# Conformer block on one core: the mixer's order of chunks, its split low parts and the first weight chunk are changed

## The chip, the cores and the metric

The kernel runs as one program on one core of a Trainium2 chip. The metric is the device time of one execution, in microseconds (us). Before the change it is 655.03 us, the median of 3 runs (653.3 to 655.46).

## The reference, cut to what matters

One layer of a hybrid block on `x` of 256 rows by 1024, fp32. There are three stages: a gated feed-forward (2816 wide), a mixer of convolution and attention, and a second feed-forward.

```python
def hybrid_layer(x, ...):
    x = x + 0.5 * swiglu(rms_norm(x, ffn1_norm), ffn1_w_gate, ffn1_w_up, ffn1_w_down)
    h = rms_norm(x, mix_norm)
    proj = h @ w_in                                  # 7 sections of 1024 columns
    conv_a, conv_b, q, k, v, gate_a, gate_b = jnp.split(proj, SPLITS, axis=-1)
    u = conv_a * jax.nn.sigmoid(conv_b)
    u = causal_depthwise_conv(u, conv_dw, conv_dw_bias)   # 31 taps
    u = jax.nn.silu(layer_norm(u, conv_ln_gain, conv_ln_bias))
    y_a = u @ w_conv_proj
    q = rms_norm(q.reshape(b, s, 16, 64), q_norm)    # per head
    k = rms_norm(k.reshape(b, s, 16, 64), k_norm)
    y_b = moba_attention(q, k, v) @ w_attn_proj
    mixed = jax.nn.sigmoid(gate_a) * y_a + jax.nn.sigmoid(gate_b) * y_b
    x = x + mixed @ w_out
    x = x + 0.5 * swiglu(rms_norm(x, ffn2_norm), ffn2_w_gate, ffn2_w_up, ffn2_w_down)
    return x
```

With 256 rows and blocks of 256, `moba_attention` is causal softmax attention within the one block: scores times 64 ** -0.5, a causal mask, softmax, times v.

## The kernel before, in words

Every large product is one `gemm` (L97): 256 rows as two halves `t`, a chunk of 512 weight columns, and k-tiles of 128. Weights come in pieces of two k-tiles (512 KB) through SyncE's queue (SP) into one of five `raw` buffers. `split` (L89) then makes two fp32r parts: ScalarE casts `raw` to `hi` (L91), and VectorE, or GpSimd where `pool_lo` is set, subtracts to get `lo` (L93). TensorE runs three matmuls for each k-tile and half: high by `hi` (L133), high by `lo` (L134), low by `hi` (L135). So a piece is 12 matmuls and a chunk of eight k-tiles is 48. A `raw` buffer is free for the next load when its low part is made. The two sums of a chunk lie in `acc`, of which there are three.

FFN 1 has 11 chunks of gate and up columns (`hTh`, `hTl` on the left) and two chunks of the down product with 22 k-tiles (`aTh`, `aTl`); FFN 2 is the same on `h2h`, `h2l`. Rows are normalised late: the product is taken on x times the gain, and the row factor `rstd` enters as the scale of the Silu (L237) and in the gated product (L260).

At the start, `start` (L533) loads x transposed, in four transfers between the first weight pieces. For each k-tile GpSimd squares it and adds it up (`sq`, L549, L551), ScalarE makes `hTh` (L552) and VectorE `hTl` (L553). The row sums are two small matmuls (`rstd_x`, L570). The natural x (1 MB, for the residual) and the constants are loaded after the second chunk (`load_rest`, L580).

The mixer has 14 chunks of `w_in`: b, a, b, a for the convolution (each 512 columns), then k, q, v, k, q, v, and four gate chunks. Each sum is turned to natural tiles and transposed on TensorE by functions kept in `later`, which run after the second piece of the next chunk. `conv` (L299) is 31 taps for each of eight tiles of 128 channels on VectorE (L313, L317), with its sum in PSUM. `pump` (L67) issues so many of its steps for each piece, behind the `anchor`, the last low part or score on VectorE. `attention` (L408) has 24 steps (score, flip and value for each of eight pairs of heads), which `side` issues at one step for each piece from the second k chunk on. A head's norm (`head_norm`, L369) is a copy and a square on ScalarE, a sum on VectorE (L380), `ms` on VectorE (L153), a power on GpSimd (L155) and a product on VectorE (L385). In the mixer's first 56 pieces 0.75 of the low parts go to GpSimd.

After the attention, ScalarE takes all eight sigmoids of both gates (L686), the chunks of `w_attn` run on `oh`, `ol`, and between the second of them and `w_conv` stands `conv_act` (L345): transposes of the normalised convolution, Silu (L359), and the parts `u2h`, `u2l`.

The tile framework orders the instructions of each engine by a simulated timeline; each engine then takes them in that order.

Of the kernel before, what the change touches and what calls it, by code (L numbers as in the profile page):

```python
# [17 lines left out]
P = 128  # L18
S = 256
# [18 lines left out]
B8_BUFS = 13  # L38
SIDE = 1.0, 1.0
PUMP = 3, 3.5, 3, 8  # L40
# [4 lines left out]
class Build:  # L45
# [16 lines left out]

    def tr(self):
# [33 lines left out]
    def gemm(self, w, c, n, kt, ah, al, pump=0, pool=0.0, first=False, split_k=None,  # L97
             side=None, before=None):
# [9 lines left out]
        for kp in sizes:  # L108
            ahead = before(k0) if before is not None else None
# [7 lines left out]
            step = 1 if first else 2
            for s in range(0, kp, step):
                e = min(s + step, kp)
                self.share += pool  # L120
                pool_lo = self.share >= 1.0
                if pool_lo:
                    self.share -= 1.0
                self.split(
                    raw[:, s * n : e * n], hi[:, s * n : e * n], lo[:, s * n : e * n], pool_lo
                )
# [22 lines left out]
    def rsqrt_mean(self, ss, n, width):  # L149
# [3 lines left out]
        nc.vector.tensor_scalar(ms, ss, 1.0 / n, EPS, ALU.mult, ALU.add)  # L153
# [17 lines left out]
    def to_T(self, src, hi, lo, k0, gain=None):  # L171
# [3 lines left out]
        ps = self.tr()
        for j in range(2):
            for t in range(2):
                nc.tensor.transpose(  # L178
                    ps[:, j * S + t * P : j * S + (t + 1) * P], src(t, j), self.ident
                )  # L180
        return self.split_T(ps, hi, lo, k0, 2, gain)
# [30 lines left out]
    def ffn(self, wgu, wd, hT, rstd_of, x, emit, tail=None, before=None, after=None):  # L212
# [9 lines left out]
        for i, n in enumerate(widths):  # L222
            last = i == len(widths) - 1
            if not last:
                if before is not None and i == 0:
                    g = self.gemm(
                        wgu, c, n, KD, ah, al, first=True, split_k=(1, 1), before=before
                    )
# [36 lines left out]
            def transp(av=av, off=off, n=n):  # L265
                for j in range(0, n // P, 2):
                    k = off // P + j
                    self.to_T(
                        lambda t, q: av[t][:, (j + q) * P : (j + q + 1) * P],
                        aTh[k // 8], aTl[k // 8], k % 8,  # L270
                    )
# [11 lines left out]
    def residual_T(self, x_new, ss, hi, lo, gain):  # L283

        def transp(c):
            for j in (0, 2):
                self.to_T(
                    lambda t, q: x_new[:, t * D + c * CH + (j + q) * P : t * D + c * CH + (j + q + 1) * P],
                    hi, lo, c * 4 + j, gain,
                )  # L290
# [8 lines left out]
    def conv(self, uT, tiles):  # L299
# [3 lines left out]
        for c0 in tiles:  # L303
# [510 lines left out]
```

## Time and profile before

| | |
|---|---|
| time, median of 3 runs | 655.03 us (653.3 to 655.46) |
| the profiled execution | 653.98 us, of which 652.2 us are the span |
| mean granted TensorE clock | 0.996 |
| TensorE busy | 640.5 us (98%), 2956 matmuls and transposes |
| VectorE busy | 413.1 us (63%) |
| ScalarE busy | 342.6 us (53%) |
| GpSimd busy | 132.5 us (20%) |
| DMA | 114.98 MB, mean 176 GB/s |

The span runs from the first to the last instruction of the profiled execution. Busy time is the union of an engine's instructions; a matmul counts as busy to its modelled end, which lies after the start of the next one, so a short wait between matmuls does not show as idle time. In lists of groups the columns are line, engine, operation, names (out, then in), shapes and count, then busy us and the mean ns of one, then the idle time of the engine just before them with what ended it. Where a stretch is tabled by windows, each engine has its busy us and, in brackets, its instructions.

### The profile page before, as it was taken

What the parts mean: (1) busy time and instruction counts of PE and PEld (TensorE: products, weight loads), DVE (VectorE), ACT (ScalarE), POOL (GpSimd) and SP (SyncE); (2) the same over time, 40 slices, a digit from 0 to 9 for tenths busy, and PEclk for the clock granted to TensorE, in tenths of its full rate; (3) what the DMA queues carried; (4) which work ended last, traced back from release to release, by engine and by line L of the source; (5) the groups of instructions that cost most, each with busy time, mean ns of one, the idle gap of its engine ahead of it and who ended that gap; (6) DMA issues with size and microseconds to landing.
All of it is one profiled execution on the core that took longest, in us unless ns stands there. A gap on an engine that the chain in (4) does not pass through costs nothing.

```text
span 652.2 us, 8131 instructions
## 1 busy us (share of the span) xinstructions
PE 640.5 (98%) x2956; PEld 519.8 (80%) x2956; DVE 413.1 (63%) x664; ACT 342.6 (53%) x512; POOL 132.5 (20%) x80
## 2 busy tenths in 40 slices
PE   7999999999999999999999999999999999999997
PEld 5788888888888888877777777788888888888886
DVE  5764636455532399999989874775754546455541
ACT  5543545354534645668665685943654535454330
POOL 6300000000025667847744400000000000000000
PEclk8999999999999999999999999999999999999999
DMA  8865655647565556444454433365655666656740
GB/s 275 315 224 164 193 193 173 216 132 233 163 213 163 183 175 219 144 153 134 156 162 130 162 124 102 130 207 179 197 171 182 193 194 182 189 162 204 206 124 32
DMA packets 33000, 114.98 MB, mean 176 GB/s; under 512 B 3648, under 2 KB 5056, under 8 KB 32960
## 3 DMA queue, kind: packets, MB, share of 16 engines
q1 hardware_dynamic: 32960, 114.46, 54.8%
q8 instruction: 23, 0.38, 0.3%
q14 instruction: 17, 0.14, 0.1%
HBM read 113.40 MB, written 1.05 MB: 175 GB/s over the span
## 4 chain that ended last, share of the span: by engine, by line
PE 90%; DVE 3%; ACT 3%; DMA 1%; issue 1%; SPq 0%; DVEq 0%; ACTq 0%
PE acc L134 28%; PE acc L133 28%; PE acc L135 28%; PE tr L178 2%; PE tr L423 1%; DMA raw<-w1gu 1%; PE tr L481 1%; DVE cv L317 1%; DVE lo L93 1%; ACT hi L91 1%; PE tr L466 1%; ACT gate L686 1%; ACT pr L445 0%; DVE hxn L385 0%; PE tr L397 0%
## 5 line engine op out<-in xcount | busy, mean ns | idle before, releaser
L91 ACT CAST hi<-raw 128x1024 fp32r<-128x1024 f32 (+1 forms) x216 | 222.9, 1037 | 242.1 <-PE acc L135 217.3
L93 DVE TENSOR_TENSOR lo<-raw,hi 128x1024 fp32r<-128x1024 f32 (+1 forms) x174 | 217.2, 1253 | 182.1 <-ACT hi L91 177.2
L93 POOL TENSOR_TENSOR lo<-raw,hi 128x1024 fp32r<-128x1024 f32 x42 | 100.9, 2421 | 219.4 <-ACT hi L91 219.2
L317 DVE SCALAR_TENSOR_TENSOR cv<-uT,cst,cv 128x255 f32<-128x255 f32 (+26 forms) x240 | 94.4, 463 | 0.1
L134 PE MATMUL acc<-lo,h1h 128*128 128x512 f32 x224 | 88.3, 394 | 0.0
L135 PE MATMUL acc<-hi,h1l 128*128 128x512 f32 x224 | 87.5, 394 | 0.0
L133 PE MATMUL acc<-hi,h1h 128*128 128x512 f32 x224 | 87.2, 394 | 0.0
L133 PE MATMUL acc<-hi,hTh 128*128 128x512 f32 x176 | 68.8, 397 | 2.9 <-ACT hi L91 2.9
L134 PE MATMUL acc<-lo,hTh 128*128 128x512 f32 x176 | 69.9, 397 | 0.7 <-DVE lo L93 0.7
L133 PE MATMUL acc<-hi,h2h 128*128 128x512 f32 x176 | 69.2, 393 | 0.0
L135 PE MATMUL acc<-hi,hTl 128*128 128x512 f32 x176 | 69.0, 393 | 0.0
L133 PE MATMUL acc<-hi,aTh 128*128 128x512 f32 x176 | 68.7, 391 | 0.0
L135 PE MATMUL acc<-hi,aTl 128*128 128x512 f32 x176 | 68.5, 389 | 0.0
L134 PE MATMUL acc<-lo,aTh 128*128 128x512 f32 x176 | 68.5, 389 | 0.0
L134 PE MATMUL acc<-lo,h2h 128*128 128x512 f32 x176 | 68.5, 390 | 0.0
L135 PE MATMUL acc<-hi,h2l 128*128 128x512 f32 x176 | 67.2, 390 | 0.0
L133 PEld LDWEIGHTS acc<-hi,h1h 128*128 128x128 f32 x224 | 42.1, 188 | 10.4 <-issue 1.3
L134 PEld LDWEIGHTS acc<-lo,h1h 128*128 128x128 f32 x224 | 42.1, 188 | 9.6 <-issue 0.7
L135 PEld LDWEIGHTS acc<-hi,h1l 128*128 128x128 f32 x224 | 42.1, 188 | 8.5 <-issue 0.3
L133 PEld LDWEIGHTS acc<-hi,hTh 128*128 128x128 f32 x176 | 33.4, 191 | 10.3 <-ACT hi L91 3.6
L134 PEld LDWEIGHTS acc<-lo,hTh 128*128 128x128 f32 x176 | 33.5, 190 | 8.9 <-DVE lo L93 2.2
L155 POOL TENSOR_TENSOR rs<-ms,neghalf 128x8 f32<-128x8 f32 (+2 forms) x13 | 17.2, 1324 | 109.7 <-DVE ms L153 109.4
(131 smaller groups left out, 783.8 us busy)
## 6 DMA issues: line engine op xcount, KB each, us to landing
raw<-w_in SPq DMA_DIRECT2D x56, 512.0 KB, 3.5
raw<-w2gu SPq DMA_DIRECT2D x44, 512.0 KB, 4.4
raw<-w1gu SPq DMA_DIRECT2D x43, 512.0 KB, 5.0
raw<-w1d SPq DMA_DIRECT2D x22, 512.0 KB, 4.2
raw<-w2d SPq DMA_DIRECT2D x22, 512.0 KB, 4.3
raw<-w_attn SPq DMA_DIRECT2D x8, 512.0 KB, 4.0
raw<-w_conv SPq DMA_DIRECT2D x8, 512.0 KB, 3.5
raw<-w_out SPq DMA_DIRECT2D x8, 512.0 KB, 4.5
```

The lines of the kernel that those rows point to most:

```text
L91: nc.scalar.copy(hi, raw)
L93: ins = eng.tensor_tensor(lo, raw, hi.bitcast(F32), ALU.subtract)
L133: nc.tensor.matmul(o, ah(k, t), wh, start=st, stop=False)
L134: nc.tensor.matmul(o, ah(k, t), wl, start=False, stop=False)
L135: nc.tensor.matmul(o, al(k, t), wh, start=False, stop=sp)
L155: nc.gpsimd.tensor_tensor(r, ms, self.neghalf[:, :width], ALU.pow)
L178: nc.tensor.transpose(ps[:, j * S + t * P : j * S + (t + 1) * P], src(t, j), self.ident)
L317: nc.vector.scalar_tensor_tensor(o, i, w, o, ALU.mult, ALU.add)
L423: nc.tensor.matmul(ps[q][:, t * P : t * P + (t + 1) * P], qT[r, b * S + t * P : b * S + (t + 1) * P], kT[r, b * S : b * S + (t + 1) * P], ...
L466: nc.tensor.transpose(ps[:, i * P : (i + 1) * P], pr[:, o : o + P], self.ident)
L481: nc.tensor.matmul(ps[q * HD : (q + 1) * HD, kt * P : S], v[:, kt * D + h * HD : kt * D + (h + 1) * HD], pT[:, o : o + n], start=kt == 0, ...
L686: last = nc.scalar.activation(g[:, sl], g[:, sl], AF.Sigmoid)
```

## The change

- **Start.** `gemm_first` replaces the first chunk: one transfer brings a k-tile's 512 weight columns and the 256 columns of x transposed that belong to it (3 KB per partition), and the sums lie in the two `cv` tiles. GpSimd's squares and the four sum matmuls go. `rstd_x` now runs after the second chunk: it loads the natural x, squares it on ScalarE (four `sum_squares`) and takes the power as elsewhere. The `ms` step of every norm goes from VectorE to ScalarE.
- **Order.** The convolution's chunks hold 256 b and 256 a columns each, so one chunk gives two tiles. They stand at places 0, 1, 5 and 9 of the 14, with k, q, v of the first heads at 2 to 4 and of the others at 6 to 8, and the gates last. The attention is issued at 0.75 steps for each piece from place 5 and 0.95 from place 9.
- **Low parts.** From the second chunk on, and in `w_attn`, every low part is GpSimd's: 60 instead of 42.
- **Head norms.** q is not normalised; its factor, with 64 ** -0.5 in it, enters as the scale of the exponential and in its bias `nb`. The row maxima lie in PSUM.
- **Convolution.** The first tap of each tile goes to ScalarE; its steps are no longer tied behind the anchor.
- **Tail.** The sigmoids of the second gate come after the Silu of `conv_act`, and `conv_act` comes ahead of the second `w_attn` chunk.

```diff
-B8_BUFS = 13
-SIDE = 1.0, 1.0
-PUMP = 3, 3.5, 3, 8
+B8_BUFS = 12
+W_IN = [
+    ("u", 0), ("u", 1), ("k", 0), ("q", 0), ("v", 0), ("u", 2), ("k", 1), ("q", 1), ("v", 1),
+    ("u", 3), ("b", 0), ("b", 1), ("a", 0), ("a", 1),
+]
+SIDE = [0] * 5 + [0.75] * 4 + [0.95] * 5
+NORM_AT = "a", 0
+PUMP = 3.5, 4
+POOL_LO = 1.0
...
-        with self.tc.issue_after(self.anchor.ins) if self.anchor else nullcontext():
+        with nullcontext():
             while self.credit >= 1 and self.bg:
...
+    def gemm_first(self, x0, w0, rest, hT):
...
+        acc = [self.cv(), self.cv()]
...
+        for k in range(KD):
+            raw = self.wp.tile([P, KP * CH], F32, tag="raw", name="raw", bufs=RAW_BUFS)
+            hi = self.wp.tile([P, KP * CH], F32R, tag="hi", name="hi", bufs=HI_BUFS)
+            lo = self.wp.tile([P, KP * CH], F32R, tag="lo", name="lo", bufs=LO_BUFS)
+            if k == 0:
+                nc.sync.dma_start(x0, self.io["x0"])
+                nc.sync.dma_start(raw[:, :CH], w0)
+                xk = x0[:, KD:]
+            else:
+                self.last_dma = nc.sync.dma_start(raw[:, : CH + S], rest[:, k - 1, :])
+                xk = raw[:, CH : CH + S]
+            g = x0[:, k : k + 1]
+            sl = slice(k * S, (k + 1) * S)
+            nc.scalar.activation(hTh[:, sl], xk, AF.Copy, scale=g)
+            nc.vector.scalar_tensor_tensor(
+                hTl[:, sl], xk, g, hTh[:, sl].bitcast(F32), ALU.mult, ALU.subtract
+            )
+            self.split(raw[:, :CH], hi[:, :CH], lo[:, :CH], False)
+            for t in range(2):
+                o, st, sp = acc[t], k == 0, k == KD - 1
+                nc.tensor.matmul(o, ah(k, t), hi[:, :CH], start=st, stop=False)
+                nc.tensor.matmul(o, ah(k, t), lo[:, :CH], start=False, stop=False)
+                nc.tensor.matmul(o, al(k, t), hi[:, :CH], start=False, stop=sp)
+        return acc
...
-        nc.vector.tensor_scalar(ms, ss, 1.0 / n, EPS, ALU.mult, ALU.add)
+        nc.scalar.activation(ms, ss, AF.Copy, bias=EPS, scale=1.0 / n)
...
-                        nc.vector.tensor_scalar(
-                            o, i, w, cst[:, C_CB + c : C_CB + c + 1], ALU.mult, ALU.add
-                        )
-                    else:
-                        nc.vector.scalar_tensor_tensor(o, i, w, o, ALU.mult, ALU.add)
...
+                    nc.scalar.activation(
+                        o, u, AF.Identity, bias=cst[:, C_CB + c : C_CB + c + 1], scale=w
+                    )
+                else:
+                    nc.vector.scalar_tensor_tensor(o, u, w, o, ALU.mult, ALU.add)
...
+            if rq is not None:
+                ms = self.tmp.tile([P, 8], F32, tag="ms8", name="ms", bufs=2)
+                nc.scalar.activation(ms, ss, AF.Copy, bias=HD * EPS)
+                nc.gpsimd.tensor_tensor(rq[:, :, t], ms, self.neghalf, ALU.pow)
+                xs.append(x)
+                continue
...
-            mx = self.tmp.tile([P, 4], F32, tag="mx", name="mx", bufs=2)
+            mx = ps[0][:, 3 * P : 3 * P + 4]
...
-            self.anchor = nc.vector.tensor_scalar(nb, mx, -scale, None, ALU.mult)
+            f = rq[b // 4].rearrange("p h t -> p (h t)")[:, (b % 4) * 4 : (b % 4) * 4 + 4]
+            self.anchor = nc.vector.scalar_tensor_tensor(
+                nb, mx, -1.0, f, ALU.mult, ALU.mult
+            )
...
-                        scale=scale, accum_out=sums[:, i : i + 1],
+                        scale=f[:, i : i + 1], accum_out=sums[:, i : i + 1],
...
+        def first():
+            return self.gemm_first(
+                x0, io["w1f"][: P * CH].rearrange("(p n) -> p n", n=CH),
+                io["w1f"][P * CH :].rearrange("(p k n) -> p k n", p=P, n=CH + S), (hTh, hTl),
+            )
...
         def rstd_x():
...
-            sums = self.tr()
-            for t in range(2):
-                nc.tensor.matmul(
-                    sums[:, t : t + 1], sq[:, t * P : (t + 1) * P], self.ones[:, :1],
-                    start=True, stop=True,
-                )
...
-                nc.sync.dma_start(cst, io["cst"])
                 nc.sync.dma_start(
                     x.rearrange("p (t d) -> p t d", t=2),
                     io["x"].rearrange("(t p) d -> p t d", p=P),
                 )
+                nc.sync.dma_start(cst, io["cst"])
+            for t in range(2):
+                for c in range(2):
+                    self.sum_squares(x, ss0, t, c)
+            return self.rms(ss0)
...
+        def conv_in(i, ba):
+            un = []
+            for t in range(2):
+                s = self.tmp.tile([P, CH], F32, tag="sg", name="sb", bufs=3)
+                nc.scalar.activation(
+                    s[:, :S], ba[t][:, :S], AF.Sigmoid, scale=rstd[:, t : t + 1]
+                )
+                u = self.tmp.tile([P, CH], F32, tag="av", name="un", bufs=3)
+                nc.vector.scalar_tensor_tensor(
+                    u[:, :S], ba[t][:, S:], rstd[:, t : t + 1], s[:, :S], ALU.mult, ALU.mult
+                )
+                un.append(u)
...
+        for cn, (what, c) in enumerate(W_IN):
+            if (what, c) == NORM_AT:
+                self.bg.append(self.conv_norm(uT, ynat))
+            acc = self.gemm(
+                w_in, cn, CH, KD, mh, ml, pump=PUMP[0], pool=POOL_LO if cn else 0,
+                side=(att, SIDE[cn]),
+            )
             if rstd is None:
                 rstd = self.rms(ss1)
...
+            if what == "u":
+                conv_in(c, acc)
+            elif what == "k":
+                self.head_norm(acc, rstd, c, kT, C_KN)
+            elif what == "q":
+                self.head_norm(acc, rstd, c, qT, C_QN, rq[c])
+            elif what == "v":
+                scaled(v, c, acc)
+            else:
+                if c == 0:
+                    gates.append(self.big(f"gate_{what}"))
+                scaled(gates[-1], c, acc)
...
-        with tc.issue_after(self.last_att.ins):
-            for g in (gb, ga):
+        def sigmoid(g, after):
+            with tc.issue_after(after.ins):
                 for i in range(4):
                     sl = slice(i * CH, (i + 1) * CH)
                     last = nc.scalar.activation(g[:, sl], g[:, sl], AF.Sigmoid)
+            return last
+        last = sigmoid(gb, self.last_att)
         for c in range(2):
-            acc = self.gemm(wb, c, CH, KD, ph, pl, pump=PUMP[3])
             if c:
                 self.drain()
-                self.conv_act(ynat, u2h, u2l, last)
+                sigmoid(ga, self.conv_act(ynat, u2h, u2l, last))
+            acc = self.gemm(wb, c, CH, KD, ph, pl, pump=PUMP[1], pool=POOL_LO)
```

## Rows read from the trace of the kernel before

**Rows 1.** The waits of TensorE by releaser, whole span: us in total, times, longest

```profile
PE acc L133 <- ACT hi L91: 2.9, 1, 2.9
PE acc L133 <- ACT u2h L365: 1.3, 1, 1.3
PE tr L466 <- DVE ms L153: 1.2, 1, 1.2
```

**Rows 2.** Line 133, first of three matmuls per k-tile: durations, first and last start

```profile
L133 PE MATMUL acc<-hi,h1h x224: 387/389/500, 197.5 to 383.3; 128*128 128x512 f32 x112
...
L133 PE MATMUL acc<-hi,hTh x176: 387/389/773, 4.8 to 135.6; 128*128 128x512 f32 x176
...
L133 PE MATMUL acc<-hi,aTh x176: 389/389/481, 136.3 to 647.4; 128*128 128x512 f32 x176
...
L133 PE MATMUL acc<-hi,h2h x176: 389/389/481, 462.6 to 587.1; 128*128 128x512 f32 x176
```

**Rows 3.** Windows: length, busy PE, PEld, DVE, ACT, POOL (counts), clock, DMA share, GB/s

```profile
0.00:10.00 10.00, 7.30 (x28) 5.71 (x28) 3.12 (x8) 4.22 (x8) 4.25 (x14) 1.00 0.71 209
10.00:20.00 10.00, 8.02 (x27) 5.86 (x27) 9.90 (x12) 8.49 (x14) 9.76 (x12) 0.83 0.84 306
20.00:30.00 10.00, 10.00 (x46) 8.28 (x47) 7.02 (x8) 4.31 (x5) 2.13 (x2) 1.00 1.00 369
```

**Rows 4.** The timeline, 3 to 12 us: start, us, instruction, idle before it

```profile
3.45 0.48 DVE L553 SCALAR_TENSOR_TENSOR hTl<-x,hTh 128x256 fp32r<-128x256 f32 x1 [2.41 <-ACT hTh L552]
...
6.46 0.68 DVE L93 TENSOR_TENSOR lo<-raw,hi 128x512 fp32r<-128x512 f32 x1
...
11.32 0.73 PE L133 MATMUL acc<-hi,hTh 128*128 128x512 f32 x2 [2.94 <-ACT hi L91]
```

**Rows 5.** Groups by shape on VectorE, 0 to 23 us: busy, mean ns, idle before

```profile
L93 DVE TENSOR_TENSOR lo<-raw,hi 128x512 fp32r<-128x512 f32 x8 | 8.3, 1072 | 0.9 <-ACT hi L91 0.8
L553 DVE SCALAR_TENSOR_TENSOR hTl<-xT,x,hTh 128x256 fp32r<-128x256 f32 x7 | 5.5, 817 | 2.8 <-ACT hTh L552 2.8
```

**Rows 6.** Groups by shape, whole span: what row norms and gating take

```profile
L260 DVE SCALAR_TENSOR_TENSOR av<-acc,rs,sg 128x512 f32<-128x512 f32 x20 | 14.2, 744 | 1.6 <-PE acc L135 1.6
...
L237 ACT ACTIVATE sg<-acc,rs 128x512 f32<-128x512 f32 x20 | 13.5, 687 | 8.7 <-PE acc L135 6.3 <-POOL rs L155 2.3
...
L161 ACT ACTIVATE junk<-x 128x512 f32<-128x512 f32 x8 | 5.0, 629 | 3.7 <-DVE x L723 2.7 <-DVE x L596 1.0
...
L155 POOL TENSOR_TENSOR rs<-ms,neghalf 128x2 f32<-128x2 f32 x3 | 3.0, 1008 | 76.2 <-DVE ms L153 76.2
```

**Rows 7.** Windows in the mixer, columns as in rows 3

```profile
240.00:285.00 45.00, 45.00 (x215) 36.91 (x214) 44.68 (x96) 24.70 (x34) 34.12 (x16) 1.00 0.56 182
285.00:330.00 45.00, 43.75 (x206) 32.80 (x205) 44.14 (x112) 33.10 (x70) 29.86 (x14) 1.00 0.42 139
330.00:385.50 55.50, 55.26 (x276) 41.44 (x276) 48.99 (x136) 38.44 (x90) 19.91 (x9) 1.00 0.41 131
```

**Rows 8.** Groups by shape, whole span: low parts, head norms, one table load

```profile
L93 DVE TENSOR_TENSOR lo<-raw,hi 128x1024 fp32r<-128x1024 f32 x166 | 208.9, 1262 | 181.1 <-ACT hi L91 176.3
L93 POOL TENSOR_TENSOR lo<-raw,hi 128x1024 fp32r<-128x1024 f32 x42 | 100.9, 2421 | 219.4 <-ACT hi L91 219.2
...
L155 POOL TENSOR_TENSOR rs<-ms,neghalf 128x8 f32<-128x8 f32 x8 | 13.1, 1636 | 7.9 <-DVE ms L153 7.5
...
L385 DVE TENSOR_TENSOR hxn<-hx,rs 128x512 f32<-128x512 f32 x8 | 10.2, 1280 | 0.0
...
L153 DVE TENSOR_SCALAR ms<-hss 128x8 f32<-128x8 f32 x8 | 5.1, 631 | 0.0
...
L445 ACT ACT_TABLE_LOAD x1 | 1.3, 1283 | 0.0
```

**Rows 9.** Line 93 on GpSimd: durations min/median/max, first and last start

```profile
L93 POOL TENSOR_TENSOR lo<-raw,hi x42: 2374/2402/2853, 190.6 to 366.7; 128x1024 fp32r<-128x1024 f32 x42
```

**Rows 10.** The waits of GpSimd, 200 to 280 us

```profile
POOL rs L155 <- DVE ms L153: 4.7, 4, 2.2
```

More of the change, by code (lines that the diff above doesn't have):

```diff
@@ L95, in split, with gemm @@
             self.anchor = ins
-    def gemm(self, w, c, n, kt, ah, al, pump=0, pool=0.0, first=False, split_k=None,
-             side=None, before=None):
+    def gemm_first(self, x0, w0, rest, hT):
+        nc = self.nc
+        acc = [self.cv(), self.cv()]
+        hTh, hTl = hT
+        ah, al = self.parts(*hT)
+        for k in range(KD):
[22 more added lines that the diff above has]
+        return acc
+    def gemm(self, w, c, n, kt, ah, al, pump=0, pool=0.0, split_k=None, side=None):
         nc = self.nc
@@ L112, in gemm @@
             lo = self.wp.tile([P, KP * CH], F32R, tag="lo", name="lo", bufs=LO_BUFS)
-            with self.tc.issue_after(ahead.ins) if ahead else nullcontext():
-                self.last_dma = nc.sync.dma_start(
-                    raw[:, : kp * n].rearrange("p (k n) -> p k n", n=n), w(c, k0, kp)
-                )
[L117 to L125, printed above, removed]
-                )
+            self.last_dma = nc.sync.dma_start(
+                raw[:, : kp * n].rearrange("p (k n) -> p k n", n=n), w(c, k0, kp)
+            )
+            self.share += pool
+            pool_lo = self.share >= 1.0
+            if pool_lo:
+                self.share -= 1.0
+            self.split(raw[:, : kp * n], hi[:, : kp * n], lo[:, : kp * n], pool_lo)
             for t in range(2):
@@ L169, in rms, with to_T @@
         return self.rsqrt_mean(s2, D, 2)
[L171 removed]
+    def to_T(self, src, hi, lo, k0, n, gain=None):
         nc = self.nc
[L175 to L181 removed]
+        for j in range(0, n, 2):
+            ps = self.tr()
+            for q in range(2):
+                for t in range(2):
+                    nc.tensor.transpose(
+                        ps[:, q * S + t * P : q * S + (t + 1) * P], src(t, j + q), self.ident
+                    )
+            self.split_T(ps, hi, lo, k0 + j, 2, gain)
     def split_T(self, ps, hi, lo, k0, nk, gain):
@@ L209, in parts, with ffn @@
         return ap(hi), ap(lo)
-    def ffn(self, wgu, wd, hT, rstd_of, x, emit, tail=None, before=None, after=None):
+    def ffn(self, wgu, wd, hT, rstd_of, x, emit, tail=None, first=None):
         nc = self.nc
@@ L224, in ffn @@
             if not last:
[L225 to L228, printed above, removed]
+                if first is not None and i == 0:
+                    g = first()
                 else:
@@ L265, in transp @@
             def transp(av=av, off=off, n=n):
[L266 to L271, printed above, removed]
+                k = off // P
+                self.to_T(
+                    lambda t, q: av[t][:, q * P : (q + 1) * P],
+                    aTh[k // 8], aTl[k // 8], k % 8, n // P,
+                )
             self.later.append(transp)
@@ L285, in transp @@
         def transp(c):
[L286 to L290, printed above, removed]
+            self.to_T(
+                lambda t, q: x_new[:, t * D + c * CH + q * P : t * D + c * CH + (q + 1) * P],
+                hi, lo, c * 4, 4, gain,
+            )
             for t in range(2):
@@ L392, in transp @@
         def transp():
-            for j in (0, 2):
+            for j in range(0, 4, 2):
                 ps = self.tr()
@@ L601, in run @@
         self.ffn(
-            w_of("w1gu", KD), w_of("w1d", KF), (hTh, hTl), rstd_x, x, emit_into(x1, x),
-            self.residual_T(x1, ss1, h1h, h1l, C_GM), before=start, after=load_rest,
+            w_of("w1gu", KD, first=1), w_of("w1d", KF), (hTh, hTl), rstd_x, x, emit_into(x1, x),
+            self.residual_T(x1, ss1, h1h, h1l, C_GM), first=first,
         )
@@ new lines, in scaled @@
+        def scaled(dst, c, acc):
+            for t in range(2):
+                nc.scalar.activation(
+                    dst[:, t * D + c * CH : t * D + (c + 1) * CH], acc[t], AF.Copy,
+                    scale=rstd[:, t : t + 1],
+                )
+        for cn, (what, c) in enumerate(W_IN):
[4 more added lines that the diff above has]
+                side=(att, SIDE[cn]),
+            )
```

205 lines of the change are left out of this document (72 added, 133 removed).

## The prediction

> **What bounds the kernel now.** I read the busy times first: TensorE is busy 98% of the span, the others far less, so the question is where the last 2% go. The list of TensorE's waits [rows 1] names few: 2.9 us on one cast of a weight piece, 1.3 us on the high part of the convolution's output, 1.2 us ahead of a transpose of the attention's probabilities. A wait is counted only past a matmul's modelled end, some 0.39 us after its start, though the next could start after 0.23 us, so each hides some 0.16 us more.
>
> The two feed-forwards check this. They hold the same products: from the first `hTh` matmul to the first `h1h` one is 197.5 - 4.8 = 192.7 us; from the first `h2h` to the last `aTh` with the three matmuls left there is 647.4 + 0.7 - 462.6 = 185.5 us [rows 2]. So FFN 1 loses 7.2 us. With 792 matmuls in 185.5 us the pace is 0.23 us each, transposes included, and a chunk of 48 takes 11.0 us. The 7.2 us lie in the start: between 0 and 20 us TensorE is busy 7.3 and 8.0 of 10 us, and its clock, at 2.4 GHz otherwise, is granted at 0.83 on average in the second stretch (part of it at 1.2 GHz), after the 2.94 us of idle time that end at 11.32 [rows 3, 4]. In that stretch VectorE is busy 9.90 of 10 us and GpSimd 9.76 [rows 3]. VectorE's two operations for a k-tile take 0.48 and 0.68 us at their shortest [rows 4], but 0.82 and 1.07 us on average beside GpSimd's squares [rows 5]. So the first chunk is held by late pieces first, then by VectorE.
>
> In the mixer the waits of [rows 1] are 2.5 us; with the hidden parts and smaller ones I put what can be won at 3 to 4 us. VectorE is busy 44.68 + 44.14 + 48.99 = 137.8 of 145.5 us between 240 and 385.5 [rows 7], 95%, ScalarE 96.2, GpSimd 83.9. The scores and `lo` parts queue behind convolution taps there.
>
> So nearly all of a gain must come out of 7.2 + 4 = 11 us, and the rest is 2.4 GHz matmul work that the change keeps.
>
> **Start.** Removed: 15 GpSimd operations and four sum matmuls. The bytes stay: 0.13 MB of x0, eight k-tiles of weights (2.10 MB) and the rest of x transposed (0.92 MB) are 3.15 MB. At the rates of [rows 3], 209 and then 306 GB/s, 2.09 MB are in by 10 us and the last k-tile by 10 + 1.06/0.306 = 13.5 us. A cast (taken like the low part), a low part of 0.68 us [rows 4] and six matmuls (1.4 us) put the end of the chunk at 16.2 us, against 4.8 + 11.0 = 15.8 without any wait. VectorE needs 0.48 + 0.68 = 1.16 us for a k-tile, less than TensorE's 1.4, so it no longer sets the pace. The least left over is 0.4 us. The most is 4.5 us: one idle stretch as in [rows 4] with a clock of 1.2 GHz behind it (17% of 10 us is 1.7 us). I take 1.7, since smaller pieces arrive more evenly than x and two k-tiles of weights by turns: a gain of 5.5 us, bounds 2.7 and 6.8.
>
> The row factor is late next. The natural x is issued on SP behind the second chunk's last piece; with five `raw` buffers and k-tiles that take one each, that piece waits for the seventh k-tile's low part, and FFN 1's third chunk is queued behind x on SP. x is complete after 3.15 + 2.10 + 1.05 = 6.30 MB: 5.15 MB by 20 us, the rest at 369 GB/s [rows 3], so at 23.1 us. Four squares (0.63 us), a power (1.01), the Silu (0.69) and the gated product (0.74) [rows 6] free a sum at 23.1 + 2.5 + 1.0 + 0.7 + 0.7 = 28.0, with handovers 28.5 to 29.5. TensorE asks for it when the second chunk and six matmuls of the third are done, 16.2 + 11.0 + 1.4 = 28.6 us, because the second chunk holds two of the three `acc` tiles. A wait of 0 to 1 us; it is in the 1.7.
>
> **Mixer, VectorE.** Low parts on GpSimd go from 42 to 52 + 8 = 60, so VectorE loses 18 of 1.26 us, 22.7 us [rows 8]; four `hxn` of 1.28, 5.1 us; eight `ms` of 0.63, 5.0 us [rows 8]. That is 33 us, and eight first taps more, out of a queue 95% full. Its in-order queue then has room, and scores and transposes come earlier.
>
> **Mixer, ScalarE.** It takes the taps, `ms` and more function tables. By the order of the program the tables change between sigmoid and exponential around chunks 5 and 9, and again in the tail (sigmoid, Silu, sigmoid, Silu): 11 loads instead of 5, six more of 1.283 us [rows 8], 7.7 us. ScalarE has 145.5 - 96.2 = 49 us free in the stretch, and casts run up to five pieces (some 13 us) ahead, so I cost this at nothing; without that cover a load delays a sum's release by 1.3 us. The Trainium skill, "ScalarE: Activation LUTs", section "What ACT_TABLE_LOAD costs", puts every switch at about 2.66 us with a drain; by that the six are 16 us, still under the free time. It advises grouping by table set, which this order breaks; the trace of before shows 1.283 us a load.
>
> **Mixer, GpSimd.** In the 13 chunks that it serves, 52 x 2.42 = 125.8 us, eight head norms of 1.64 are 13.1 [rows 8], and its wait for `ms`, 4.7 us for four [rows 10], 9.6 for eight: 148.5 us. TensorE has for these 13/14 of 383.3 + 2 - 197.5 [rows 2], some 174 us. It keeps up on average. Where two head norms follow each other (q, then v) its load is 9.7 + 3.3 + 2.4 = 15.4 us a chunk against some 12, 7 us over two chunks, against a lead of up to four pieces (11 us). Hidden, but the norms' powers and `ms` now share a queue with every low part.
>
> **Tail.** `conv_act` and its Silu start four sigmoids earlier and a chunk earlier, so the 1.3 us wait should go.
>
> **Sum.** I take 2.5 us of the mixer's 3 to 4, bounds 0 and 4. Profiled execution 653.98 - 5.5 - 2.5 = 646.0 us. The median of the runs shown lies 1.05 above it: **647.0 us**. All waits gone gives 653.98 - 11 + 1.05 = 644.0.
>
> **Rivals.**
> - **GpSimd becomes the bound (slower).** All low parts stand in one in-order queue. It decides when a low part takes (174 - 22.7)/52 = 2.91 us; the longest of 42 took 2.85, the median 2.40 [rows 9]. Against it: those 2.40 were measured beside a full VectorE. For it: VectorE's own low part stretches beside GpSimd (0.68 to 1.07, [rows 4, 5]), so the two do block each other, and GpSimd's share rises. At 3.2 us it costs 52 x 3.2 + 22.7 - 174 = 15 us: 653.98 - 5.5 + 15 + 1.05 = 664.5 us. The Trainium skill, "SBUF — State Buffer", section "Who interferes with whom", says that GpSimd and a VectorE operation with two SBUF inputs lock one port pair, and that whichever starts second blocks fully; the stretched low parts agree, and the steady 2.40 us say that VectorE mostly lost. Chance 0.14.
> - **The start is bound by bytes and by x.** If the first pieces stall as now, or x comes 3 us later, 4.5 us stay: 649.8 us. Chance 0.14.
> - **The mixer's waits move.** A table load or a power that stands ahead of a cast or a low part in its queue, or a score out of time, costs each some 1 to 1.4 us as in [rows 1]; with four to six of them the mixer loses 1.5 us instead of winning 2.5: 651.0 us, up to 654. Chance 0.17.
> - **Nothing moves**, because gains and new waits cancel: 653 to 657. Chance 0.07.
> - My forecast: 0.48.
>
> About 0.3% (2.0 us) is what a measurement of this kernel can tell from no change. Faster holds the forecast, the start's rival and most of the moving waits: 0.48 + 0.14 + 0.13 = 0.75. Same: 0.07 + 0.03 = 0.10. Slower: 0.14 and a remainder of 0.01, 0.15. The range reaches from 642.8, just under all waits gone, to 655.0, and leaves out the GpSimd case and part of the last.
>
> **What would show it.** Start: first `h1h` matmul at about 192 instead of 197.5; no cast or low part in TensorE's waits before 20 us; VectorE well under 9 of 10 us between 10 and 20; the clock at 1.00 there. Row factor: a wait of the third chunk on VectorE's gated product would be the rival. Mixer: VectorE near 75% between the same places, GpSimd near 85%, low parts at 2.4 us; the time from the first `h1h` to the first `h2h` matmul falls from 265 to some 262.5 us; no wait on `u2h`. The prediction fails if GpSimd's low parts top TensorE's waits, if the granted clock drops in the mixer, or if x is late by more than 3 us.

## The result, and the profile after

The changed kernel takes 646.86 us (median of 4 runs, 646.5 to 647.54) against 654.45 us (4 runs) for the kernel before, a ratio of 0.9884 with a 95% interval of 0.9867 to 0.9902. The profiled execution is 646.76 us with a span of 644.9, against 653.98 and 652.2 before.

First the starts of the first of the three matmuls of each k-tile (now L165), which cut the span into stages: first and last start, by stage.

```profile
L165 PE MATMUL acc<-hi,h1h x224: 387/389/501, 191.9 to 377.1; 128*128 128x512 f32 x112
...
L165 PE MATMUL acc<-hi,aTh x176: 389/389/476, 130.7 to 640.1; 128*128 128x512 f32 x176
L165 PE MATMUL acc<-hi,h2h x176: 387/389/479, 455.3 to 579.8; 128*128 128x512 f32 x176
```

Against [rows 2] the first `h1h` matmul comes 197.5 - 191.9 = 5.6 us earlier: that is the start. From there to the first `h2h` matmul, the mixer, it was 265.1 us and is 455.3 - 191.9 = 263.4: 1.7 us. From there to the end of the span it is 189.6 us in both. The sum is the 7.3 us by which the span is shorter.

The three windows of the start, columns as in [rows 3]:

```profile
0.00:10.00 10.00, 8.92 (x36) 7.39 (x37) 5.17 (x12) 6.81 (x13) 1.44 (x10) 1.00 0.82 272
10.00:20.00 10.00, 9.53 (x42) 7.54 (x41) 6.98 (x10) 6.04 (x10) 0.00 (x0) 1.00 0.94 318
20.00:30.00 10.00, 10.00 (x46) 8.29 (x45) 5.81 (x8) 7.85 (x16) 1.64 (x1) 1.00 0.98 369
```

TensorE is busy 8.92 and 9.53 us where it was 7.30 and 8.02, its granted clock stays at 1.00 (2.4 GHz), VectorE falls from 9.90 to 6.98 us and GpSimd from 9.76 to nothing. The groups of VectorE between 0 and 23 us show why it has room:

```profile
L102 DVE TENSOR_TENSOR lo<-raw,hi 128x512 fp32r<-128x512 f32 x8 | 5.5, 692 | 0.6 <-ACT hi L100 0.5
...
L126 DVE SCALAR_TENSOR_TENSOR hTl<-raw,x,hTh 128x256 fp32r<-128x256 f32 x7 | 3.4, 485 | 1.9 <-ACT hTh L125 1.8
```

The low part of a k-tile takes 692 ns on average, not 1072, and that of x 485, not 817 [rows 5]: the shortest times of before [rows 4] are now the mean. What follows in the timeline is the row factor:

```profile
22.19 0.63 ACT L193 ACTIVATE junk<-x 128x512 f32<-128x512 f32 x1 [1.33 <-DMA x<-x]
...
27.56 1.27 ACT L271 ACTIVATE sg<-cv,rs 128x512 f32<-128x512 f32 x2 [0.81 <-POOL rs L187]
```
```profile
25.89 1.64 POOL L187 TENSOR_TENSOR rs<-ms,neghalf 128x2 f32<-128x2 f32 x1 [23.81 <-ACT ms L185]
```

The natural x has landed by 22.19 us, and TensorE shows no wait on the Silu or the gated product behind it. The power took 1.64 us because a low part on VectorE had begun just before it (the last section has the rows).

The mixer's windows, as in [rows 7], with their sum:

```profile
240.00:285.00 45.00, 45.00 (x212) 34.38 (x211) 38.69 (x118) 35.33 (x68) 37.48 (x18) 1.00 0.52 168
285.00:330.00 45.00, 45.00 (x228) 34.72 (x227) 27.84 (x81) 38.72 (x77) 34.71 (x17) 1.00 0.44 141
330.00:385.50 55.50, 55.50 (x264) 41.57 (x264) 28.96 (x92) 39.10 (x78) 37.52 (x17) 1.00 0.50 161
sum 145.50, PE 145.50 PEld 110.66 DVE 95.49 ACT 113.16 POOL 109.71; mean PE 48.50 PEld 36.89 DVE 31.83 ACT 37.72 POOL 36.57
```

VectorE is busy 95.5 of 145.5 us (66%), before 137.8; GpSimd 109.7 (75%); TensorE shows no idle time there at all. The waits of TensorE over the whole span, and GpSimd's low parts:

```profile
PE tr L568 <- DVE idle L565: 1.1, 1, 1.1
PE acc L165 <- ACT u2h L398: 0.8, 1, 0.8
PE acc L166 <- DVE lo L102: 0.5, 1, 0.5
```
```profile
L102 POOL TENSOR_TENSOR lo<-raw,hi x60: 2355/2400/2846, 193.2 to 394.9; 128x1024 fp32r<-128x1024 f32 x60
```

Of the mixer's two waits in [rows 1], 1.2 us ahead of a transpose is gone and 1.3 us on `u2h` is 0.8: together 1.7 us, as much as the mixer gained, so what else moved there cancels out. (The 1.1 us lies ahead of the warm-up matmuls. The 0.5 us on a low part ends at 17.69 us, at the second chunk's first piece; the prediction had expected no such wait before 20 us.) Where the 0.8 us come from is in ScalarE's timeline of the tail:

```profile
389.05 0.37 ACT L220 CAST oh<-tr 128x256 fp32r<-128x256 f32 x1 [2.09 <-PE tr L524]
389.44 1.28 ACT L697 ACT_TABLE_LOAD   x1
390.73 2.20 ACT L697 ACTIVATE gate_b<-gate_b 128x512 f32<-128x512 f32 x4
...
396.67 0.59 ACT L364 COPY ynat<-tr 128x512 f32<-128x512 f32 x1
400.74 0.21 ACT L185 ACTIVATE ms<-mv 128x1 f32<-128x1 f32 x1 [3.48 <-DVE mv L370]
...
404.42 1.28 ACT L392 ACT_TABLE_LOAD   x1
406.06 1.94 ACT L392 ACTIVATE z<-tr,cst 128x256 f32<-128x256 f32 x4 [0.35 <-PE tr L385]
407.87 0.63 ACT L398 CAST u2h<-z 128x512 fp32r<-128x512 f32 x1
```

Attention's last output (389.05), gate_b's sigmoids, the convolution's norm (copies to 396.67, statistics to 400.74), the Silu table, the Silu and the `u2h` cast follow each other on ScalarE, and the last of them ends just too late.

### The profile page after: what moved, and what is told of

Its sections match the earlier page's. It is cut to its first block, busy times and chain, and to the rows that moved or that the text cites. A ratio compares the mean times of both kernels' runs of the same rounds, so it can differ in the third digit from the quotient of the medians.

```text
span 644.9 us, 8142 instructions
## 1 busy us (share of the span) xinstructions
PE 638.5 (99%) x2952; PEld 517.1 (80%) x2952; DVE 371.6 (58%) x625; ACT 365.9 (57%) x549; POOL 163.1 (25%) x83
## 3 DMA queue, kind: packets, MB, share of 16 engines
HBM read 113.40 MB, written 1.05 MB: 177 GB/s over the span
## 4 chain that ended last, share of the span: by engine, by line
PE 67%; ACT 0%; DVE 0%; issue 0%; DVEq 0%
PE acc L165 20%; PE acc L166 20%; PE acc L167 20%; PE tr L463 2%; PE tr L524 1%; PE tr L211 1%; PE tr L509 1%; PE tr L438 1%; PE tr L359 0%; PE tr L649 0%; ACT z L392 0%; PE tr L385 0%; ACT u2h L398 0%; DVE un L640 0%; DVE ot L748 0%
## 5 line engine op out<-in xcount | busy, mean ns | idle before, releaser
L102 DVE TENSOR_TENSOR lo<-raw,hi 128x1024 fp32r<-128x1024 f32 (+1 forms) x156 | 186.6, 1199 | 169.7 <-ACT hi L100 165.3
L102 POOL TENSOR_TENSOR lo<-raw,hi 128x1024 fp32r<-128x1024 f32 x60 | 142.9, 2404 | 213.2 <-ACT hi L100 213.2
L347 DVE SCALAR_TENSOR_TENSOR cv<-uT,cst,cv 128x255 f32<-128x255 f32 (+28 forms) x240 | 95.4, 469 | 10.6 <-ACT cv L343 10.4
L165 PE MATMUL acc<-hi,h1h 128*128 128x512 f32 x224 | 88.3, 399 | 0.2 <-DVE un L640 0.2
L165 PE MATMUL acc<-hi,h2h 128*128 128x512 f32 x176 | 69.1, 393 | 0.0
L165 PE MATMUL acc<-hi,aTh 128*128 128x512 f32 x176 | 68.8, 391 | 0.0
L166 PE MATMUL acc<-lo,hTh 128*128 128x512 f32 x160 | 62.4, 390 | 0.5 <-DVE lo L102 0.5
L165 PE MATMUL acc<-hi,hTh 128*128 128x512 f32 x160 | 62.2, 392 | 0.0
L167 PE MATMUL acc<-hi,hTl 128*128 128x512 f32 x160 | 62.1, 389 | 0.0
L165 PEld LDWEIGHTS acc<-hi,h1h 128*128 128x128 f32 x224 | 42.1, 188 | 11.2 <-issue 2.0
L167 PEld LDWEIGHTS acc<-hi,aTl 128*128 128x128 f32 x176 | 33.0, 188 | 6.9
L165 PEld LDWEIGHTS acc<-hi,h2h 128*128 128x128 f32 x176 | 33.0, 188 | 6.8
L165 PEld LDWEIGHTS acc<-hi,aTh 128*128 128x128 f32 x176 | 33.0, 188 | 6.8
```

The source lines that it names most:

```text
L102: ins = eng.tensor_tensor(lo, raw, hi.bitcast(F32), ALU.subtract)
L165: nc.tensor.matmul(o, ah(k, t), wh, start=st, stop=False)
L166: nc.tensor.matmul(o, ah(k, t), wl, start=False, stop=False)
L167: nc.tensor.matmul(o, al(k, t), wh, start=False, stop=sp)
L347: nc.vector.scalar_tensor_tensor(o, u, w, o, ALU.mult, ALU.add)
```

## The experiments

Ratios are to the kernel before on the same chip. The first `h1h` start and the mixer's length (first `h1h` to first `h2h` start) are read from the profile of each, in us. Before: 197.5 and 265.1; changed: 191.9 and 263.4. Times are medians, the last two columns those of one execution: it lies 0.8 us under the median in e3, 1.7 over it in e8 and 3.5 over it in e9, elsewhere within 0.3.

| kernel | us | ratio, 95% interval | `h1h` | mixer |
|---|---|---|---|---|
| e1 new start alone | 648.83 | 0.9931 (0.9918 to 0.9944) | 192.2 | 265.2 |
| e2 new mixer alone | 651.58 | 0.9966 (0.9954 to 0.9978) | 196.9 | 263.4 |
| e3 before, no squares | 652.0 | 0.9973 (0.996 to 0.9986) | 194.6 | 265.2 |
| e4 after, squares on | 649.6 | 0.9937 (0.9925 to 0.9949) | 194.8 | 263.4 |
| e5 after, old tail | 649.71 | 0.9944 (0.9931 to 0.9957) | 191.6 | 266.6 |
| e6 after, 42 low parts | 652.04 | 0.9975 (0.9967 to 0.9984) | 192.7 | 268.0 |
| e7 GpSimd loaded, free | 648.77 | 0.9928 (0.9916 to 0.9941) | 194.2 | 263.4 |
| e8 after, old chunk order | 650.23 | 0.9958 (0.9946 to 0.9971) | 192.3 | 268.1 |
| e9 GpSimd loaded, chained | 677.22 | 1.0346 (1.03 to 1.0393) | 193.0 | 296.3 |
| e10 fewer turns | 645.63 | 0.9881 (0.9866 to 0.9896) | 192.9 | 261.3 |
| e11 norm earlier | 647.35 | 0.9909 (0.9894 to 0.9923) | 192.8 | 263.4 |
| e12 low parts alone | 654.33 | 1.0005 (0.9994 to 1.0017) | 196.7 | 265.7 |

**e1 and e2: the two halves.** e1 is the kernel before with `gemm_first`, the natural x and its row factor; e2 is the changed kernel with the old `start`, squares and sum matmuls.

> The kernel before with the new first chunk and the new row factor alone; mixer and tail as before. Theory: the start gives 5.5 us by itself, a ratio of 0.9915, with the first h1h matmul at about 192 us and the mixer's 265 us unchanged. Rival: start and mixer only pay together (the mixer's waits shift when it begins earlier), then under 4 us or the mixer's length moves by over 1 us.

> The changed kernel with the start of before (squares on GpSimd, x transposed in four transfers, two-k-tile pieces). Theory: the mixer gives 1.7 us by itself, a ratio of 0.9974, first h1h matmul at about 197.5 us and 263.4 us from there to the first h2h matmul. Rival: it gives nothing alone (within 0.5 us) or 3 us and more.

The halves add up: 0.9931 x 0.9966 = 0.9897, near 0.9884, and each half's stage is as long as in the whole change to 0.3 us. So they can be studied apart.

**e3 and e4: what in the start.** e3 takes GpSimd's squares out of the old start (the row factor then comes from the natural x as in the change); e4 puts them into the new one, where nobody reads them.

```
e3 -   nc.gpsimd.tensor_tensor(sq[:, sl], src, src, ALU.mult)
   -   if j: nc.gpsimd.tensor_tensor(sq[:, :S], sq[:, :S], sq[:, sl], ALU.add)
e4 +   nc.gpsimd.tensor_tensor(self.sq[:, sl], xk, xk, ALU.mult)
   +   if k: nc.gpsimd.tensor_tensor(self.sq[:, :S], self.sq[:, :S], self.sq[:, sl], ALU.add)
```

> The kernel before without GpSimd's squares and the four sum matmuls; the row factor from the natural x after the second chunk, first sums in the two cv tiles; weight pieces and transfers of x transposed as before. Theory A (VectorE, slowed by GpSimd, holds the first chunk): 3 to 5 us faster. Theory B (the uneven arrival of pieces holds it, with the 2.9 us idle and the low clock behind it): under 1.5 us faster, the idle stretch and a granted clock under 0.9 between 10 and 20 us stay.

> The changed kernel with the 15 squares and sums on GpSimd put back beside the first chunk (their result is not used). Theory A: VectorE's 1.16 us for a k-tile become 1.9 us, over TensorE's 1.4, so the first chunk ends some 3 us later, ratio to the changed kernel 1.004 to 1.006. Theory B: under 0.7 us slower.

In the profiled executions both give 2.9 us: the start falls from 197.5 to 194.6 in e3 and rises from 191.9 to 194.8 in e4. In e4 VectorE is full again and its low part is back at 1067 ns, with TensorE waiting on it six times (columns of windows, groups and waits as above):

```profile
10.00:20.00 10.00, 8.68 (x33) 5.55 (x32) 10.00 (x11) 5.18 (x9) 8.53 (x10) 1.00 0.77 241
```
```profile
L102 DVE TENSOR_TENSOR lo<-raw,hi 128x512 fp32r<-128x512 f32 x8 | 8.5, 1067 | 0.8 <-ACT hi L100 0.7
```
```profile
PE cv L136 <- DVE lo L102: 1.8, 6, 0.4
```

In e3 the idle stretch on a cast stays, yet the clock in the second window is 1.00:

```profile
10.00:20.00 10.00, 8.44 (x36) 6.73 (x37) 8.82 (x15) 8.64 (x15) 0.00 (x0) 1.00 0.94 348
```
```profile
PE cv L136 <- ACT hi L94: 2.8, 1, 2.8
```

So of the start's 5.6 us, 2.9 are VectorE relieved of GpSimd's company, and the other 2.7, which e4 keeps, are pieces that arrive in the order of use. The 2.9 hold where the clock holds. e3's twelve executions spread from 650.30 to 655.27 us, the five shortest at a mean granted clock of 0.999 or 1.000, the longest at 0.991, and their median is only 1.5 us under that of before. So with the idle stretch left in, part of the gain seems to be lost in most executions (only one of them has a trace), and neither theory holds alone. The change's own four executions stay within 1.1 us.

**e5, e6 and e8: one part of the mixer undone.** e5 restores the tail (both gates' sigmoids first, then the convolution's end inside the second `w_attn` chunk); e6 the 42 low parts; e8 the four convolution chunks in front, attention beside the last seven.

```
e5 -   last = sigmoid(gb, self.last_att)          # and conv_act ahead of chunk 1
   +   sigmoid(gb, self.last_att)
   +   last = sigmoid(ga, self.last_att)          # and conv_act behind its matmuls
e6 -POOL_LO = 1.0                                 # pool=POOL_LO if cn else 0; w_attn too
   +POOL_LO = 0.75                                # pool=POOL_LO; none in w_attn
e8 -SIDE = [0] * 5 + [0.75] * 4 + [0.95] * 5
   +SIDE = [0] * 7 + [1.0] * 7                    # W_IN: u 0..3, then k q v, k q v, b b a a
```

> The changed kernel with the tail of before: all eight sigmoids first, conv_act behind the second w_attn chunk. Theory: the wait on u2h was cut by the new tail; it comes back from 0.8 to some 1.3 us with its low part behind it, 0.8 to 1.2 us slower than the changed kernel. Rival: the tail hides itself (the attention and the convolution end earlier now anyway), within 0.4 us.

> The changed kernel with 0.75 of the w_in low parts on GpSimd and those of w_attn on VectorE, as before: 42 instead of 60. Theory: VectorE's queue fills again (22 us more), a wait of a score or a transpose comes back, 0.5 to 1.5 us slower than the changed kernel. Rival: VectorE has room either way since head norms and first taps went, within 0.4 us.

> The changed kernel with the four convolution chunks first and the attention from the seventh place on at one step per piece, as before; all else changed. Theory: the order spreads VectorE's taps, so without it the mixer is 0.5 to 1.5 us slower. Rival: the order costs as much in turns of TensorE and table loads as it wins, within 0.4 us, or the old order is faster.

Each was expected to cost about 1 us and costs more than the mixer's whole gain: 3.2, 4.6 and 4.7 us in the profiled executions, the last about 3 by e8's median (an estimate: 4.7 less the 1.7 us by which its profiled execution lies over it). All three show one new wait in the same place, ahead of the transposes that wait for the Silu's `z`; the lines of e5, e6 and e8:

```profile
PE tr L385 <- ACT z L392: 2.2, 1, 2.2
```
```profile
PE tr L385 <- ACT z L392: 2.5, 1, 2.5
```
```profile
PE tr L385 <- ACT z L392: 2.4, 1, 2.4
```

What e5 adds ahead of it is gate_a's sigmoids; the Silu's table is loaded at 406.59, not 404.42. In e6 attention's last output comes at 393.30 instead of 389.05, in e8 at 399.88. And the wait is not the whole bill. Windows of e5 behind it:

```profile
408.00:412.00 4.00, 2.28 (x8) 1.75 (x9) 2.85 (x4) 3.70 (x8) 0.00 (x0) 0.74 0.75 240
412.00:416.00 4.00, 4.00 (x17) 3.20 (x16) 1.29 (x2) 2.86 (x6) 0.00 (x0) 0.84 0.29 112
416.00:420.00 4.00, 4.00 (x19) 3.34 (x18) 1.26 (x2) 1.36 (x2) 0.00 (x0) 1.00 0.33 91
```

The granted clock is 0.74 and 0.84 there, part of the time at 1.2 GHz, so the first `u2h` matmuls run long (up to 795 ns instead of 389). In e6 the clock is 0.83 from 410 to 420 us, in e8 0.84 from 400 to 410. With what the slower matmuls add, and other waits beside it (in e8 one of 1.4 us ahead of the attention's value products), a wait of 2.2 to 2.5 us ends as 3.2 to 4.7. The fall does not come in every execution: four of e8's six take 649.85 to 650.26 us at a mean granted clock of 0.999 or 1.000, the other two, the profiled one among them, 651.88 and 652.34 us at 0.997.

**e7 and e9: is GpSimd near its bound?** One more GpSimd product behind each of its low parts, read by nobody. In e7 it depends on nothing; in e9 it reads the parts just made and so must stand in line.

```
e7 +   nc.gpsimd.tensor_tensor(self.waste, self.waste, self.waste, ALU.mult)   # 128x256
e9 +   nc.gpsimd.tensor_tensor(self.waste, lo[:, :512].bitcast(F32), hi[:, :512].bitcast(F32), ALU.mult)
```

> The changed kernel with one product of 128x256 in place on GpSimd behind each of its 60 low parts (its result is not used), which takes 0.6 to 1.0 us by the squares of before, so a low part costs 3.0 to 3.4 us of GpSimd. Theory: the point from which GpSimd bounds the mixer is 2.91 us; here 5 to 25 us slower than the changed kernel, with GpSimd's low parts at the head of TensorE's waits. Rival: the pieces run far enough ahead, under 2 us slower.

> The changed kernel with one more GpSimd product (128x512, inputs the low and high part just made, output read by nobody) behind each low part that GpSimd makes; it must stand in line there, unlike in the run before. Estimate of one product: half of a low part of 128x1024, 1.2 us, so GpSimd needs about 3.6 us for each low part instead of 2.40. If the prediction's bound holds (GpSimd decides from 2.91 us per low part), 52 to 56 parts x (3.6 - 2.91) = 36 to 39 us longer, TensorE waits on low parts of GpSimd: 683 to 686 us. If the bound lay further out (GpSimd's line has slack that the sum didn't see), less than 10 us longer.

e7 misses its aim: with no inputs to wait for, 27 of the 60 products ran in the first 30 us and the rest by 66 us, ahead of the mixer, and all it shows of the time is e4's effect once more (start 194.2, mixer unchanged). e9 answers. Its GpSimd groups and TensorE's longest waits:

```profile
L102 POOL TENSOR_TENSOR lo<-raw,hi 128x1024 fp32r<-128x1024 f32 x60 | 144.0, 2404 | 179.3 <-ACT hi L100 179.2
L106 POOL TENSOR_TENSOR waste<-lo,hi 128x512 f32<-128x512 f32 x60 | 81.7, 1362 | 0.5
```
```profile
PE tr L442 <- DVE hxn L430: 7.4, 2, 5.0
PE acc L170 <- POOL lo L102: 7.0, 12, 1.0
```

At 2.40 + 1.36 = 3.77 us per low part the mixer is 32.9 us longer. The rival's formula with 3.77 gives 52 x 3.77 + 22.7 - 174 = 45 us. So the bound is real, and lies a little further out: taken as linear, 3.77 - 32.9/52 = 3.1 us per low part instead of 2.91. This is a rough estimate from one point: the profiled execution is the slowest of four (the median is 3.5 us less, which gives 3.2), and its granted clock was 0.92 and 0.96 between 240 and 330 us, so part of the 32.9 us is the clock's. The change stands 0.7 us under it with its 2.40. The longest waits are on `hxn`, that is on the head norms' powers in the same queue, as the prediction had named.

**e10 and e11: the last 0.8 us.** e10 joins attention's steps; e11 queues the convolution's norm a chunk earlier.

```
e10 -  score(b) / yield / flip(b - 1) / yield / value(b - 1) / yield       # 24 turns
    +  flip(b) / yield / value(b), score(b + 2) / yield                    # 18 turns
    -SIDE = [0] * 5 + [0.75] * 4 + [0.95] * 5
    +SIDE = [0] * 5 + [0.5625] * 4 + [0.7125] * 5
e11 -NORM_AT = "a", 0
    +NORM_AT = "b", 1
```

> The changed kernel with attention in 18 turns between the pieces instead of 24: the values of one head pair and the scores of the pair after the next share a turn; its rate is cut from 0.75 and 0.95 turns per piece to 0.5625 and 0.7125, so that it ends at the same piece. Theory: each turn of TensorE away from the large matmuls and back costs 0.12 to 0.15 us, 41 of them became 57, and that gave back a part of the waits won. Then 6 turns fewer are worth 0.7 to 0.9 us: the mixer takes 262.6 instead of 263.4, 646.0 us in all. Rival: the turns cost nothing, or the scores that stand longer before their use hold the buffers up and a wait appears: no change or up to 3 us longer.

> The changed kernel with the convolution's norm queued one chunk earlier (ahead of the second gate_b chunk rather than the first gate_a chunk), so that it can end before the first gate sigmoids. Theory: the wait of 0.8 us on u2h is what is left of the mixer's tail; Silu starts earlier, the wait goes, 0.8 us faster: mixer 262.6, 646.0 us. Rival 1: Silu is held by the gate sigmoids and the matmuls of the weight stream in front of it, not by the norm: same within 0.3 us. Rival 2: the norm's copies now stand between attention's operations on ScalarE and make attention end later, which cost 3 to 5 us in the three runs before where the end slipped: 649 to 651 us.

e11's edit moves nothing: every engine's instructions stand in the order of the changed kernel, so it says nothing of the tail. It serves as a repeat of the changed kernel: the mixer is again 263.4, the start 0.9 us later, and the ratio 0.0025 higher, which is how far two such measurements differ here. Against it, on the same chip, e10 is 1.7 us faster (645.26 to 645.79 against 647.15 to 647.67), and the best of all kernels run; its mixer takes 261.3. But the reason given for it is not tested in that form: counted in the trace, the groups of small operations between large matmuls were 42 before, 58 after the change, and are 59 in e10, since the transposes stand in more groups. What e10 did join are the value and score products: 16 separate runs of them before, 22 after the change, 17 in e10. A step from a large matmul into such a run takes 0.32 us and out of it 0.31, into a transpose 0.23 and out of it 0.03 (medians, start to start), so these runs are the costly ones. The steps into, within, out of and just behind them sum to 32.6 us in the changed kernel (166 steps) and 29.9 in e10 (159); less seven large steps of 0.227 this makes 1.2 us (an estimate). The wait on `u2h` falls to 0.5, another 0.3. Where the last 0.6 us come from stays open. For the change itself the count says little: its six more runs have fewer switches between values and scores inside them, 4 instead of 12.

**e12: GpSimd's low parts alone**, in the kernel before.

```
-  b = self.gemm(w_in, 2 * c, ..., pool=0.75)          # w_attn: no pool
+  b = self.gemm(w_in, 2 * c, ..., pool=1.0 if c else 0)   # all others 1.0, w_attn too
```

> One part alone: the kernel before, with its start, its order of chunks and its tail, but all 60 low parts of 13 mixer chunks and of the two attention chunks on GpSimd, as the change has them (42 before). Theory 1: VectorE's relief carries the mixer's gain by itself; attention and the convolution's norm end earlier, the two waits of 1.2 and 1.3 us shrink, the mixer takes 263 to 264 us instead of 265.1, 652.5 to 653.5 us in all (before taken at 654.4). Theory 2 (from the three runs in which one part undone cost 3 to 5 us): the parts hang together, and low parts alone do not give the mixer's gain; the tail's order is unchanged and the wait on u2h stays at 1 to 1.5 us, 265 us for the mixer, same within 0.3%. Theory 3: with VectorE relieved and ScalarE still without the taps, GpSimd becomes late beside the norms: waits on its low parts, over 266 us.

No gain, 265.7 us in the mixer. The wait on `u2h` shrinks to 0.4, but another grows to 2.6 us; by the windows around it the clock falls to 0.50 (1.2 GHz) behind it:

```profile
310.00:316.00 6.00, 5.33 (x30) 4.29 (x29) 6.00 (x14) 1.78 (x9) 6.00 (x3) 1.00 0.48 146
316.00:320.00 4.00, 1.85 (x9) 1.19 (x7) 4.00 (x10) 2.73 (x7) 4.00 (x3) 1.00 0.59 211
320.00:324.00 4.00, 3.43 (x11) 1.71 (x11) 4.00 (x12) 4.00 (x7) 2.54 (x2) 0.65 0.43 131
324.00:328.00 4.00, 4.00 (x11) 3.13 (x11) 1.78 (x5) 1.77 (x3) 4.00 (x3) 0.50 0.39 133
```
```profile
314.22 0.41 ACT L445 ACTIVATE pr<-pr,nb 128x128 f32<-128x128 f32 x1 [6.26 <-DVE nb L441]
```

ScalarE waited 6.26 us for a score's bias from VectorE, which is full from 310 to 324 us (third busy time), with GpSimd full beside it until 320. Part of it is not work but waiting for GpSimd. The bias `nb` (L441) takes 0.14 us at its shortest, and here 2.10; it begins while a low part runs on GpSimd and ends 0.03 us after that low part, at 314.18:

```profile
311.76 4.75 POOL L93 TENSOR_TENSOR lo<-raw,hi 128x1024 fp32r<-128x1024 f32 x2
```
```profile
312.08 2.10 DVE L441 TENSOR_SCALAR nb<-mx 128x4 f32<-128x4 f32 x1
```
```profile
L441 DVE TENSOR_SCALAR nb<-mx x8: 138/497/2096, 286.3 to 385.9; 128x4 f32<-128x4 f32 x8
```

`ms` and `hxn` show the same (up to 2.11 and 2.54 us, 0.15 and 0.67 at their shortest). The change has taken most of these out of GpSimd's way: `ms` is ScalarE's, four of eight `hxn` are gone, and `nb` reads its maxima from PSUM:

```profile
L482 DVE SCALAR_TENSOR_TENSOR nb<-tr,rq x8: 153/159/169, 257.8 to 370.6; 128x4 f32<-128x4 f32 x8
```

Five of these eight run beside a low part, and none is longer for it. Whether it is PSUM or the other form of the operation that frees it is not separated, and no run undoes these edits by themselves; that they are what lets 60 low parts pay is argued from these rows. Taps and scores still queue on VectorE in e12; in the change the taps are spread and partly on ScalarE.

## Why the prediction came out right

The forecast was 647.0 us and 646.86 was measured; the profiled execution was put at 646.0 and is 646.76. That the medians agree to 0.14 us is luck in part: the mixer gave 0.8 us less than forecast, and the median lies 0.1 us over the profiled execution where 1.05 was added. By its steps:

- **Start, -5.5 forecast, -5.6 measured.** The 1.7 us that it left over was a choice between 0.4 and 4.5, not a sum, so the last tenths are luck. Its means are right: the first chunk's last matmul starts at 16.35 us (16.2 forecast for its end), the clock stays at 1.00, VectorE is off its limit; only the wait of 0.5 us on a low part was not expected. e3 and e4 give the split that the prediction did not make: 2.9 for VectorE beside GpSimd, 2.7 for arrival.
- **Row factor, in time, as forecast**, by two errors that cancel: x landed about 1 us earlier than 23.1 us, the power took 1.64 us and not the 1.01 of [rows 6], which is a mean of unlike ones (0.70 and 1.62). The gated product began at 28.29 us.
- **Mixer, -2.5 forecast, -1.7 measured, within its bounds of 0 and 4.** The step that failed is the tail's: "the 1.3 us wait should go". 0.8 us of it stay. The rest of the wait list came off in full; the hidden parts that the prediction added to it brought nothing net. Two slips in its sums move nothing: 2.94 + 1.7 is 4.6 and not 4.5, twice 4.7 is 9.4 and not 9.6.
- **VectorE and GpSimd.** VectorE fell to 66%, not 75%, GpSimd rose to 75%, not 85%, at 2.40 us a low part: both have more room than forecast. The 33 us that the prediction takes from VectorE were in part not work: the means of 0.63 for `ms` and 1.28 for `hxn` hold waits for GpSimd's low parts (0.15 and 0.68 us at their shortest before). That the two engines block each other is in the prediction, but for the mixer only as GpSimd's risk; e12 shows it as VectorE's cost, which the change avoids.
- **Table loads**, 13 and not 11, at 1283 ns each, cost nothing in the stretch as argued; the one ahead of the Silu stands in the tail's chain.
- **Rivals.** GpSimd's bound did not bind, but e9 shows that it exists and, by the rough estimate there, that 0.7 to 0.8 us more per low part would have met it. The rival of moved waits was worth more than it looked: e5, e6, e8 and e12 are what it describes, each with a wait of 2 us or more and, in the profiled execution, a clock at 1.2 GHz for a time behind it. Not one of the three parts undone leaves the mixer at or under its 265.1 us of before.
- **Open:** 0.6 of the 2.1 us by which e10's mixer is shorter. The q norm in the exponential, the maxima in PSUM, `ms` on ScalarE and the first taps there were not undone by themselves.

## What to carry to other kernels

Where TensorE is busy 98% of the span, cost a change by the list of its waits first: here it gave the net gain, and nothing came on top for hidden parts. Look at how far each late chain is from TensorE's own time: here one that ended 0.8 us late cost 0.8 us, but waits of 2.2 to 2.5 us cost 3 to 5 in executions in which the clock fell too. The order, the share of work and the tail had to be moved together: each of them taken back lost more than all had won, and the low parts alone won nothing. Work that feeds only a later sum is not free on an idle GpSimd when VectorE stands on the path beside it. And before long work goes to GpSimd, look at the short VectorE operations on the path: one of 0.14 us took 2.10 behind a low part.

## What was not expected of the hardware

- The granted clock fell behind single waits of TensorE in the middle of full work: after 2.2 us in e5 to 0.74 and 0.84 in stretches of 4 us, after 2.6 us in e12 to 0.50. In e3's start an idle stretch of 2.8 us left the stretch from 10 to 20 us at 1.00, while other executions of e3 show a lower mean clock (down to 0.991). Why the clock falls in one execution and not in another is not settled.
- GpSimd and VectorE hold each other up, and in these traces it is the one that begins second that takes longer. VectorE: `nb` and `ms` in e12, 0.15 us and then 2.1; in the start its low part of half the columns, 692 and then 1067 ns. GpSimd: e7's product of 128x256 takes 0.61 to 0.62 us in all 20 cases in which VectorE runs nothing at its start, and up to 1.68 in the other 40. GpSimd's long low part mostly goes first and keeps its 2.4 us (means of 2404 ns in the change and in e9, 2421 before); the one of 2.85 in the change began behind an `hxn`.
- GpSimd's power of one shape, 128x2, takes two times, which the mean of 1.01 in [rows 6] hides: one of 1.62 and two of 0.70. In eight traces (before, the change, e1, e3, e7, e9, e10, e12) the long one is that ahead of which a low part of VectorE had begun, the short one that with VectorE idle at its start. In the change:

```profile
25.73 2.36 DVE L102 TENSOR_TENSOR lo<-raw,hi 128x1024 fp32r<-128x1024 f32 x2 [0.78 <-ACT hi L100]
```
```profile
195.96 0.71 POOL L187 TENSOR_TENSOR rs<-ms,neghalf 128x2 f32<-128x2 f32 x1 [0.33 <-ACT ms L185]
```

The first is the low part ahead of the power at 25.89 us; beside the second VectorE does nothing.
